# Hybrid streaming encoder step: output stores moved from ScalarE's queue to SP's, second x tile loaded and scaled behind the first weights

## The chip, the cores and the metric

The kernel runs on one core of one Trainium2 chip. A core has a matrix engine (PE), three elementwise engines (DVE, ACT for ScalarE, POOL for GpSimd) and SP, which here only issues DMAs. Each engine takes its own instructions in the order in which the program lists them. The metric is the device time of one execution in microseconds (us); less is better.

## The reference

One layer is applied to 1024 prompt rows and, with cached state, to 64 sample rows, each of width 1024, all in float32. Cut to what matters:

```python
def _layer(x, ...):
    h = _rms_norm(x, norm1_g)
    parts = jnp.split(h @ w_in, ...)           # 1024 x 3080
    ...                                        # three mixers: gated delta net, gated MLP, windowed attention
    x = x + jnp.concatenate([o_a, o_b, o_c], axis=-1) @ w_out
    h = _rms_norm(x, norm2_g)
    x = x + (jax.nn.silu(h @ w_gate) * (h @ w_up)) @ w_down      # 1024 x 2816, twice, and 2816 x 1024
    return x, caches and states
```

The change touches the first lines (the norm of the first rows of x) and the last (the stores of the final x, `y_p` for the prompt and `y_s` for the sample).

## The kernel before

**Precision.** A float32 product is made of three reduced-precision ones: an operand is split into a rounded high part (`acopy` to `h`, on ACT) and the remainder (a subtraction to `l`, on DVE), and PE multiplies high by high, high by low and low by high. Weights pass from the loaded tile `wr` into `hw` and `lw`.

**Start.** Rows are treated in three segments. For the first segment `x_load` (L251) loads row tiles of 128 x 1024 into `xs`, `Weights.load` (L119) loads pieces of `w_in` into `wr` (three buffers), and `x_stat` (L290) makes the reciprocal root mean square of each row: Square with a sum on ACT (L293), then a multiply-add (L287) and a power (L288) on POOL. The first two row tiles are scaled in place on DVE (L317), transposed on PE (L303), multiplied by the norm's gain and split. `W.run(1)` splits the first piece of weights. A scheduler sets the order of each engine ahead of the run, up to the last stage (`manual_schedule`, L1888), where the engines keep the written order as it stands.

**End.** The down projection of the feed-forward block uses a Strassen-like scheme of seven products instead of eight. Its inner dimension is cut into blocks (`KB`, six of them, the last with a single piece), and in each block the sample rows and then four pairs of prompt row tiles (here pair 0 to 3) are worked off. In a pair there are seven steps (`STEPS`, here n0 to n6), each with an operand tile `w` of its own that SP loads from DRAM (`a_load`, L1764, from `hd`). In the last block a step is three matmuls, and an operand is 128 KB. Steps n0, n1 and n2 give partial sums: ACT copies them out of PSUM (L86) and POOL adds them to the output tile `yf` (L1817). Steps n3 to n6 finish the four half tiles of the pair: DVE adds them (`y_add`, L92), and `y_out` (L1782) stores the 128 x 512 half tile, 256 KB. PSUM banks tie the steps together: n2 and n4 write on in a bank that ACT has just copied out, n6 in one that DVE has just added.

**What orders the loads of the end.** `fetch` (L1866) writes one `a_load` into the program after each step. It keeps at most nine operands named in `AL` ; the sample operands of the six blocks are never taken out of `AL`, so in the last block the written lead of a load over its step is three steps. On the chip a load waits for its buffer to be free, for an older DMA of its semaphore to have landed, and for what stands ahead of it on SP, and for nothing else.

Of the kernel before, what the change touches and what calls it, by code (L numbers as in the profile page):

```python
# [12 lines left out]
ALU = mybir.AluOpType  # L13
# [40 lines left out]
def hybrid_step(ctx, tc, x_prompt, x_sample, cache_k, cache_v, st_gdn, st_conv, norm1_g, w_in, conv_w, a_log,  # L54
# [3 lines left out]
    V, A, G, T, SP = nc.vector, nc.scalar, nc.gpsimd, nc.tensor, nc.sync  # L58
# [17 lines left out]
    def sb(p, shape, tag, dt=F32, bufs=None):  # L76
        return p.tile(shape, dt, tag=tag, name=tag, bufs=bufs)

    def ax():
        return pp.tile([128, 512], F32, tag="ax", name="ax", bufs=6)  # L80
# [167 lines left out]
    def x_rows(s, t):  # L248
        t0, np_, ns = SEGS[s]
        return (x_prompt[0, t0 + 128 * t:t0 + 128 * t + 128, :], 128) if 128 * t < np_ else (x_sample[0], 64)  # L250

    xs_tiles = {}

    def x_load(s, t, q=G):
        src, r = x_rows(s, t)
        x = sb(xp, [128, DM], "xs", bufs=3)
        q.dma_start(out=x[:r], in_=src)
        xs_tiles[s, t] = x
# [7 lines left out]
    prm1 = sb(gp, [128, 390], "tr", bufs=9)  # L266
    A.dma_start(out=prm1[0:8, 0:128], in_=norm1_g[0].rearrange("(k p) -> k p", p=128))
    W.load()
    W.load()
    x_load(0, 1)  # L270
    W.load()
    x_load(0, 2, SP)
    SP.dma_start(out=cst[:, 192:], in_=cst_in[:, 192:])
# [10 lines left out]
    def gpow(out, in_, a, b, e):  # L284
        n = in_.shape[-1]
        r = in_.shape[0]
        G.tensor_scalar(out=out, in0=in_, scalar1=a, scalar2=b, op0=ALU.mult, op1=ALU.add)  # L287
        G.tensor_tensor(out=out, in0=out, in1=e[:r, :n], op=ALU.pow)  # L288

    def x_stat(x, r):  # L290
        jk = sb(wp, [128, DM], "xt2", BF16, bufs=2)
        ss = sb(cp, [128, 1], "ss", bufs=4)
        A.activation(out=jk[:r], in_=x[:r], func=AF.Square, accum_out=ss[:r])  # L293
        gpow(ss[:r], ss[:r], 1.0 / DM, EPS, mhalf)
        return ss
# [16 lines left out]
            acopy(h, t[:, :, :r])  # L312
            tt(xl[:, 4 * j:4 * j + 4, c0:c0 + r], t[:, :, :r], h.bitcast(F32), ALU.subtract)

    rstd = [x_stat(xs_tiles[0, t], 128) for t in range(2)]
    for t in range(2):
        first = V.tensor_scalar(out=xs_tiles[0, t], in0=xs_tiles[0, t], scalar1=rstd[t], scalar2=None, op0=ALU.mult)  # L317
    pb = ax()
    T.transpose(pb[:, :8], prm1[0:8, 0:128], ident[0:8, 0:8])
    g1T = sb(cp, [128, 8], "g1T")  # L320
    V.tensor_copy(out=g1T, in_=pb[:, :8])
    ctx.enter_context(tc.issue_after(first.ins))
    W.run(1)
    prm = sb(gp, [128, 390], "tr", bufs=9)
    SP.dma_start(out=prm[0:8, 0:128], in_=norm2_g[0].rearrange("(k p) -> k p", p=128))
    SP.dma_start(out=prm[8:9, 0:128], in_=gdn_g)
# [1330 lines left out]
    D, AL, yf = {}, {}, {}  # L1657
# [124 lines left out]
    def y_out(t, h):  # L1782
        c = slice(512 * h, 512 * h + 512)
        dst = y_p[0, 128 * t:128 * t + 128, c] if t < 8 else y_s[0, :, c]
        A.dma_start(out=dst, in_=yf[t][:dst.shape[0], c])


    STEPS = ((0, "Y", ((0, 0, 0),)), (1, "Z", ((1, 1, 0),)), (2, "Y", ((0, 1, 0),)), (3, "X", ((0, 0, 1),)),
# [2 lines left out]
    def pair_steps(b, p):  # L1791
        kps, banks = KB[b], {}

        def step(n, bank, adds):
            fresh = bank not in banks
            if fresh:
                banks[bank] = mmb() if bank == "X" else ax()
            ps, a = banks[bank], AL.pop((b, p, n))
            m = 0
            for k, kp in enumerate(kps):  # L1800
                bh, bl = D[kp][RIGHT[n]]
                for l, r in ((a[:, 2 * k], bh), (a[:, 2 * k], bl), (a[:, 2 * k + 1], bh)):
                    T.matmul(ps, l, r, start=fresh and m == 0, stop=m == 3 * len(kps) - 1,  # L1803
                             skip_group_check=not fresh)
                    m += 1
                if p == 3 and n in LAST:
                    PT.give(D[kp][LAST[n], "h"], D[kp][LAST[n], "l"])
            WS.give(a)

            def add():  # L1810
                for i, j, done in adds:
                    t = PAIRS[p][2 + i]
                    if b + 1 == len(KB) and not done:
                        slot = WS.take()
                        c = slice(512 * j, 512 * j + 512)
                        acopy(block(slot), ps)
                        G.tensor_tensor(out=yf[t][:, c], in0=block(slot), in1=yf[t][:, c], op=ALU.add)  # L1817
                        WS.give(slot)
                        continue
                    y_add(t, j, ps)  # L1820
                    if done and b + 1 == len(KB):
                        y_out(t, j)
            later.append(add)
# [3 lines left out]
    def sample_steps(b):  # L1827
        kps = KB[b]

        def step(j):  # L1830
            ps, v = ax(), AL[b]
            m, last = 0, 4 * len(kps) - 1
            for k, kp in enumerate(kps):
                for i in range(2):
                    for w in D[kp]["B%d%d" % (i + 1, j + 1)]:
                        mm(ps, v[:, 2 * k + i], w, m == 0, m == last)
                        m += 1
            if j:
                WS.give(v)

            def add():
                slot = WS.take()
                tmp = block(slot)[:64]
                c = slice(512 * j, 512 * j + 512)
                acopy(tmp, ps[64:128, :])
                tt(yf[8][:64, c], ps[0:64, :], yf[8][:64, c], ALU.add)
                tt(yf[8][:64, c], tmp, yf[8][:64, c], ALU.add)
                WS.give(slot)
                if b + 1 == len(KB):
                    outs.append(lambda: y_out(8, j))  # L1850
            later.append(add)

        return [lambda j=j: step(j) for j in range(2)]
# [134 lines left out]
```

## Time and profile before

| | us |
|---|---|
| median of 3 runs | 1350.33 (1349.97 to 1350.61) |
| the profiled execution, its own time | 1349.63 |
| its span, first to last instruction | 1347.9 |
| PE busy in the span | 1311.6 |
| granted clock of PE, mean | 0.996 |

A row of the timeline reads: start and length in us, engine, line of the kernel, operation, tile written <- tiles read, shapes, how many instructions were put together (x3), and in brackets the idle time of the engine just before it and who ended it. ACTq and SPq are the two engines' instruction queues as they issue DMAs. A row of the DMA issues ends with the size of one and the median time from issue to landing.

### The profile page before, as it was taken

What the parts mean: (1) busy time and instruction counts of PE and PEld (TensorE: products, weight loads), DVE (VectorE), ACT (ScalarE), POOL (GpSimd) and SP (SyncE); (2) the same over time, 40 slices, a digit from 0 to 9 for tenths busy, and PEclk for the clock granted to TensorE, in tenths of its full rate; (3) what the DMA queues carried; (4) which work ended last, traced back from release to release, by engine and by line L of the source; (5) the groups of instructions that cost most, each with busy time, mean ns of one, the idle gap of its engine ahead of it and who ended that gap; (6) DMA issues with size and microseconds to landing.
All of it is one profiled execution on the core that took longest, in us unless ns stands there. A gap on an engine that the chain in (4) does not pass through costs nothing.

```text
span 1347.9 us, 26489 instructions
## 1 busy us (share of the span) xinstructions
PE 1311.6 (97%) x9922; PEld 1169.9 (87%) x9922; DVE 936.8 (70%) x2190; ACT 635.4 (47%) x1629; POOL 175.3 (13%) x250
## 2 busy tenths in 40 slices
PE   6999999999999999998999999999999988999997
PEld 6988888888878887788999999999999976777784
DVE  5887866756577675588866776667766687767764
ACT  7677455562555553546545554455544532222202
POOL 3101120100111110100000000000000333232104
PEclk9999999999999999999999999999999999999999
DMA  8975654434455573152533553345433499666645
GB/s 263 350 259 190 230 181 162 153 126 159 163 172 173 205 263 113 73 194 81 160 115 125 177 159 124 110 137 177 147 122 116 148 340 326 220 220 239 214 144 199
DMA packets 183075, 243.63 MB, mean 181 GB/s; under 512 B 14523, under 2 KB 133792, under 8 KB 182946
## 3 DMA queue, kind: packets, MB, share of 16 engines
q1 hardware_dynamic: 174754, 229.34, 51.6%
q10 hardware_dynamic: 6704, 8.36, 1.7%
q0 software_dynamic: 1488, 4.23, 1.0%
q8 instruction: 78, 1.28, 0.4%
q14 instruction: 51, 0.42, 0.1%
HBM read 160.92 MB, written 81.04 MB: 180 GB/s over the span
## 4 chain that ended last, share of the span: by engine, by line
PE 82%; DVE 6%; issue 6%; POOL 2%; DMA 2%; ACT 2%; POOLq 0%; ACTq 0%; DVEq 0%
PE ax L1490 29%; PE mm L95 25%; PE ax L95 11%; PE ax L1803 8%; PE mm L1490 5%; DVE x L92 2%; PE mm L1803 1%; DMA hd<-w 1%; PE ax L303 1%; PE ax L531 1%; DVE tr L89 1%; POOL x L1817 1%; PE ax L866 1%; POOL ssk L288 1%; DMA xs<-in_x_prompt_dram 0%
## 5 line engine op out<-in xcount | busy, mean ns | idle before, releaser
L1490 PE MATMUL ax<-x,w 128*128 128x256 f32 (+1 forms) x2552 | 358.6, 287 | 0.0
L1490 PEld LDWEIGHTS ax<-x,w 128*128 128x128 f32 x2552 | 334.2, 190 | 0.3 <-ACT x L86 0.2
L92 DVE TENSOR_TENSOR w<-w,w 128x512 fp32r<-128x512 f32 (+1 forms) x242 | 164.4, 687 | 88.4 <-PE ax L1490 52.7
L95 PE MATMUL mm<-xh,hw 128*128 128x384 f32 (+1 forms) x432 | 151.6, 351 | 0.0
L95 PE MATMUL mm<-xl,hw 128*128 128x384 f32 (+1 forms) x432 | 142.7, 330 | 0.0
L95 PE MATMUL mm<-xh,lw 128*128 128x384 f32 (+1 forms) x432 | 142.2, 329 | 0.0
L1803 PE MATMUL ax<-x,w 128*128 128x512 f32 x480 | 132.7, 401 | 7.8 <-DVE x L92 7.6
L92 DVE TENSOR_TENSOR x<-ax,x 128x512 f32<-128x512 f32 (+1 forms) x144 | 98.3, 687 | 58.6 <-PE ax L1803 48.3
L1803 PEld LDWEIGHTS ax<-x,w 128*128 128x128 f32 x480 | 91.7, 193 | 31.4 <-DVE x L92 11.4
L1490 PE MATMUL ax<-xr,w 128*128 128x288 f32 x616 | 116.1, 296 | 1.2 <-DVE s L92 1.2
L86 ACT ACTIVATE w<-w 128x512 fp32r<-128x512 f32 x154 | 94.9, 624 | 38.5 <-PE mm L1490 14.9
L1490 PEld LDWEIGHTS ax<-xr,w 128*128 128x128 f32 x616 | 94.9, 188 | 1.5 <-DVE s L92 1.5
L95 PEld LDWEIGHTS mm<-xh,hw 128*128 128x128 f32 x432 | 81.1, 188 | 9.6 <-issue 6.8
L86 ACT ACTIVATE s<-ax 128x256 f32<-128x256 f32 (+1 forms) x132 | 52.0, 394 | 75.7 <-PE ax L1490 75.2
L95 PEld LDWEIGHTS mm<-xl,hw 128*128 128x128 f32 x432 | 81.5, 189 | 0.8 <-issue 0.3
L95 PEld LDWEIGHTS mm<-xh,lw 128*128 128x128 f32 x432 | 81.0, 188 | 0.6
L1803 PE MATMUL ax<-f,w 128*128 128x512 f32 x220 | 72.5, 399 | 2.8 <-ACT w L86 1.5
L89 DVE SCALAR_TENSOR_TENSOR tr<-tr,cw 128x384 f32<-128x384 f32 (+1 forms) x108 | 64.1, 594 | 12.7 <-ACT tr L86 11.3
L1706 POOL TENSOR_TENSOR w<-x 128x512 f32<-128x512 f32 x6 | 8.8, 1463 | 488.4 <-PE ax L1490 442.2
L1490 PE MATMUL mm<-x,w 128*128 128x256 f32 (+1 forms) x528 | 70.5, 289 | 0.0
L1490 PEld LDWEIGHTS mm<-x,w 128*128 128x128 f32 x528 | 67.9, 190 | 0.2 <-issue 0.2
L95 PE MATMUL mm<-hw,xh 128*128 128x256 f32 (+1 forms) x216 | 62.6, 294 | 0.0
(360 smaller groups left out, 2489.9 us busy)
## 6 DMA issues: line engine op xcount, KB each, us to landing
hd<-e SPq DMA_DIRECT2D x140, 256.0 KB, 2.4
w<-hd SPq DMA_DIRECT2D x140, 256.0 KB, 4.3
lw<-wk SPq DMA_DIRECT2D x46, 512.0 KB, 4.5
hw<-wk SPq DMA_DIRECT2D x46, 512.0 KB, 3.7
wr<-in_w_in_dram SPq DMA_DIRECT2D x28, 512.0 KB, 5.9
wk<-hw SPq DMA_DIRECT2D x25, 512.0 KB, 3.8
wk<-lw SPq DMA_DIRECT2D x25, 512.0 KB, 3.9
w<-in_ffn_w_gate_dram SPq DMA_DIRECT2D x44, 256.0 KB, 3.3
```

The lines of the kernel that those rows point to most:

```text
L86: return A.activation(out=out, in_=in_, func=AF.Copy, scale=scale)
L89: return V.scalar_tensor_tensor(out=out, in0=in0, scalar=s, in1=in1, op0=op0, op1=op1)
L92: return V.tensor_tensor(out=out, in0=in0, in1=in1, op=op)
L95: return T.matmul(out, lhsT, rhs, start=start, stop=stop)
L288: G.tensor_tensor(out=out, in0=out, in1=e[:r, :n], op=ALU.pow)
L303: T.transpose(b[k // 4][:, (k % 4) * r:(k % 4) * r + r], x[:r, k * 128:k * 128 + 128], ident[:r, :r])
L531: T.transpose(b[u // 4][:, (u % 4) * 128:(u % 4) * 128 + 128], src(u).rearrange("p h i -> p (h i)"), ident)
L866: T.transpose(PTp[0:r0 + cnt, j, kv, :], P[:, kv, 128 * j:128 * j + r0 + cnt], ident)
L1490: T.matmul(ps[:, :NB[c]], a[:, k, :], b[:, k, :], start=first and i == 0, stop=i == 11, skip_group_check=not first)
L1706: eng.tensor_tensor(out=block(t), in0=a, in1=b, op=ALU.subtract)
L1803: T.matmul(ps, l, r, start=fresh and m == 0, stop=m == 3 * len(kps) - 1, skip_group_check=not fresh)
L1817: G.tensor_tensor(out=yf[t][:, c], in0=block(slot), in1=yf[t][:, c], op=ALU.add)
```

## The change

Three edits. `y_out` issues its stores on SP instead of on ACT. The second x tile is loaded on SP, between the first and the second piece of weights, instead of on POOL after the second. And the second tile's statistics and scaling are written behind the split of the first weights (`W.run(1)`), while `issue_after` now ties later DVE work to the first tile's scaling.

```diff
     W.load()
+    x_load(0, 1, SP)
     W.load()
-    x_load(0, 1)
     W.load()
...
-    rstd = [x_stat(xs_tiles[0, t], 128) for t in range(2)]
-    for t in range(2):
-        first = V.tensor_scalar(out=xs_tiles[0, t], in0=xs_tiles[0, t], scalar1=rstd[t], scalar2=None, op0=ALU.mult)
+    def x_first(t):
+        rstd = x_stat(xs_tiles[0, t], 128)
+        return V.tensor_scalar(out=xs_tiles[0, t], in0=xs_tiles[0, t], scalar1=rstd, scalar2=None, op0=ALU.mult)
+
+    first = x_first(0)
     pb = ax()
...
     ctx.enter_context(tc.issue_after(first.ins))
     W.run(1)
+    x_first(1)
...
-        A.dma_start(out=dst, in_=yf[t][:dst.shape[0], c])
+        SP.dma_start(out=dst, in_=yf[t][:dst.shape[0], c])
```

PE's order is the same before and after. On SP, in the last block, this is the stretch from pair 0's operand for n4 to pair 1's operand for n2, before:

```order
L1764 DMA w_16313<-hd 128x256
L1764 DMA w_16321<-hd 128x256
L1764 DMA w_16329<-hd 128x256
L1764 DMA w_16336<-hd 128x256
L1764 DMA w_16343<-hd 128x256
L1764 DMA w_16350<-hd 128x256
```

The same stretch of SP now, up to the first sample stores; w_16329 is what pair 0's n6 multiplies, w_16336, w_16343, w_16350 and w_16359 are pair 1's n0 to n3, x_14319 and x_14341 are pair 0's two output tiles:

```order
L1767 DMA w_16313<-hd 128x256
L1767 DMA w_16321<-hd 128x256
L1788 DMA out_dram<-x_14319 128x512
L1767 DMA w_16329<-hd 128x256
L1788 DMA out_dram<-x_14341 128x512
L1767 DMA w_16336<-hd 128x256
L1788 DMA out_dram<-x_14319 128x512
L1767 DMA w_16343<-hd 128x256
L1788 DMA out_dram<-x_14341 128x512
L1767 DMA w_16350<-hd 128x256
L1767 DMA w_16359<-hd 128x256
L1788 DMA out_dram<-x_14467 64x512 x2
```

The four stores of a pair, which wait for the sums after n3, n4, n5 and n6, now stand each ahead of an operand that is needed three steps on: the n6 operand of the same pair, then n0, n1 and n2 of the next. In the other pairs the order is the same, except that the sample stores come only here.

On ACT, before, the stores stood among the copies out of PSUM (pair 0's stores and pair 1's three copies):

```order
L1785 DMA out_dram<-x_14319 128x512
L1785 DMA out_dram<-x_14341 128x512
L1785 DMA out_dram<-x_14319 128x512
L1785 DMA out_dram<-x_14341 128x512
L86 ACTIVATE w_16356<-ax 128x512
L1785 DMA out_dram<-x_14467 64x512 x2
L86 ACTIVATE w_16367<-ax 128x512
L86 ACTIVATE w_16375<-ax 128x512
```

The same place of ACT now, with pair 1's three copies and the first two of pair 2:

```order
L86 ACTIVATE w_16356<-ax 128x512
L86 ACTIVATE w_16367<-ax 128x512
L86 ACTIVATE w_16375<-ax 128x512
L86 ACTIVATE w_16413<-ax 128x512
L86 ACTIVATE w_16422<-ax 128x512
```

ACT holds the copies alone, one behind the other; no store stands between them any more.

At the start of ACT's program (xs are the two x tiles, hw_154 and hw_148 the first piece of weights, hw_222 the second), as a piece of the difference:

```order
 L293 ACTIVATE xt_138,ss<-xs 128x1024
-L293 ACTIVATE xt_143,ss<-xs 128x1024
-L86 ACTIVATE hw_154<-wr 128x264 x4
+L86 ACTIVATE hw_148<-wr 128x264 x4
+L293 ACTIVATE xt_160,ss<-xs 128x1024
 L86 ACTIVATE hw_222<-wr 128x264 x4
```

The second tile's Square now stands behind the first weights' four copies; in the same way DVE's second scaling (L317) moved behind the four `lw` subtractions (L92). POOL's order keeps both multiply-adds (L287) ahead of both powers (L288), so the first tile's power still follows the second tile's Square. On SP the second x tile stands ahead of the second piece of weights, and the fourth piece, which waits for `lw`, moved ahead of five small parameter loads.

## Prediction

> **What bounds the kernel now.** I read the page first, then stages, then the timeline of the two ends. On the page PE is busy nearly throughout, so a change elsewhere counts only where PE waits.
>
> ```profile
> PE 1311.6 (97%) x9922; PEld 1169.9 (87%) x9922; DVE 936.8 (70%) x2190; ACT 635.4 (47%) x1629; POOL 175.3 (13%) x250
> ```
>
> Three stages of the end, as busy time of each engine in the stretch (then granted clock, DMA share, GB/s):
>
> ```profile
> 1310.00:1320.00 10.00, 9.99 (x44) 7.54 (x42) 6.33 (x9) 2.99 (x5) 1.67 (x2) 1.00 0.19 53
> 1326.00:1332.00 6.00, 4.13 (x18) 2.76 (x17) 2.77 (x4) 1.08 (x2) 2.92 (x3) 1.00 0.94 320
> 1338.00:1344.00 6.00, 5.12 (x19) 2.96 (x17) 2.38 (x5) 1.68 (x3) 3.82 (x3) 1.00 0.43 159
> ```
>
> Up to 1320 PE has no hole. In the last block it has: 1.9 us of six in the second row, 0.9 in the third. So what is moved there is on the path. Who makes the holes (ACT's rows, then PE's wait):
>
> ```profile
> 1320.80 3.49 ACTq L1785 DMA_DIRECT2D out_dram<-x  x4
> 1324.42 0.60 ACT L86 ACTIVATE w<-ax 128x512 f32<-128x512 f32 x1 [4.51 <-DVE x L92]
> 1326.04 1.19 ACTq L1785 DMA_DIRECT2D out_dram<-x  x2
> 1332.40 1.09 ACT L86 ACTIVATE w<-ax 128x512 f32<-128x512 f32 x2 [4.03 <-DMA out_dram<-x]
> PE ax L1803 <- ACT w L86: 3.2, 4, 1.7
> ```
>
> ACT's copies stand behind stores that wait for DVE's sums, and PE lost 3.2 us to late copies, in four waits, the longest behind the two sample stores at 1326.04. That is the most that freeing ACT can give back.
>
> SP's side, as its queue's rows and its waits:
>
> ```profile
> 1295.63 35.91 SPq L1764 DMA_DIRECT2D w<-hd  x28
> 1305.44 0.32 SPq L1764 DMA_DIRECT2D w<-hd  x1
> 1320.23 3.35 SPq L1764 DMA_DIRECT2D w<-hd  x7
> SPq L1764 <- DVE x L92: 3.7, 2, 2.9
> 1322.12 1.20 PE L1803 MATMUL ax<-f,w 128*128 128x512 f32 x4 [0.51 <-DVE x L92]
> ```
>
> The 28 rows are the 28 operands of the last block. The seventh, pair 0's n6, was issued at 1305.44 and used at 1322.12: a lead of 16.7 us in which any landing hides. SP does keep its order: the 14th load waited 2.9 us for a sum on DVE, until 1320.23, and the next six came in a row behind it, one per 0.48 us (3.35 / 7).
>
> **The stores on SP: what is late next.** Now each pair's store after n3 stands ahead of the same pair's n6 operand, and the stores after n4, n5, n6 ahead of the next pair's n0, n1, n2. A store waits for its sum, and with it everything behind: the lead of 16.7 us shrinks to three steps, less the sum, two issues and a landing. The path of one round, in rows of the last pair:
>
> ```profile
> 1336.51 1.20 PE L1803 MATMUL ax<-f,w 128*128 128x512 f32 x4 [0.17 <-DVE x L92]
> 1339.33 0.96 PE L1803 MATMUL ax<-f,w 128*128 128x512 f32 x3 [0.46 <-ACT w L86]
> 1341.08 0.69 DVE L92 TENSOR_TENSOR x<-mm,x 128x512 f32<-128x512 f32 x1 [2.87 <-PE mm L1803]
> 1341.80 3.07 ACTq L1785 DMA_DIRECT2D out_dram<-x  x4
> 1342.79 0.96 PE L1803 MATMUL ax<-f,w 128*128 128x512 f32 x3 [0.17 <-DVE x L92]
> 1344.53 0.34 ACTq L1785 DMA_DIRECT2D out_dram<-x  x1
> ```
>
> These are pair 2's n6 (with the first matmul of pair 3), pair 3's n2, the sum after n3, the first store, n6, and the last store. Call L the time from an operand's issue to its landing.
> - From n2's start to the store after n3: 1341.80 - 1339.33 = 2.47. Then 0.48 to the load's issue, then L. So n6 starts 2.95 + L after n2; before, 1342.79 - 1339.33 = 3.46. The load ends last as soon as L is over 0.51.
> - From n6's start to the store after it: 1344.53 - 1342.79 = 1.74; 0.48; L. So the next n2 starts 2.22 + L after n6; before, 1339.33 - 1336.51 = 2.82. The load ends last as soon as L is over 0.60.
> - A round is then 5.17 + 2L; before, 1342.79 - 1336.51 = 6.28. The operands of n0 and n1 follow earlier stores, and those of n3 to n5 come 0.48 apart behind n2's while PE takes 0.7 a step; none of them ends a path. The sample stores add two issues ahead of pair 1's n4; its n6, which waits for its own load, hides them.
> - Start: the first store was issued at 1320.80 and moves to SP at the same time. Pair 0's n6 starts at 1320.80 + 0.48 + L. Three rounds later pair 3's n6 starts at 1321.28 + L + 3 x (5.17 + 2L) = 1336.79 + 7L. It stood at 1342.79, so **the end moves by 7L - 6.00**. Behind n6 all is as before: sum, store, landing, now SP's.
>
> The gain on ACT is inside this: the copies are early, but n2 waits for its operand anyway.
>
> **How long is L.** Landing times in three stretches: loads of 128 KB with nothing else, the crowded end, and the last four stores:
>
> ```profile
> w<-hd SPq DMA_DIRECT2D x7, 128.0 KB, 2.1
> w<-hd SPq DMA_DIRECT2D x17, 128.0 KB, 3.8
> out_dram<-x ACTq DMA_DIRECT2D x4, 256.0 KB, 2.0
> ```
>
> No row has a 128 KB load right behind a 256 KB store in a calm stretch. Below, L is the 2.1 of a lone load: +8.7. Above, the 3.8 of the crowd, where seven loads a round are issued back to back beside the stores: +20.6. The new round moves 4 x 256 and 7 x 128 KB, 2.0 MB, in some 10 us, 200 GB/s, nearer to the row at 159 than to that at 320, so I go by the lone load plus its wait behind the store: 262 KB at 320 GB/s are 0.82 us, less the 0.48 between the issues, 0.3. **L = 2.4, and the end moves by 7 x 2.4 - 6.0 = +10.8 us.**
>
> Two rules of the Trainium skill bear on this, and they point apart. Its page "Perfetto Trace Analysis", section "DMA Optimizations", advises giving inputs one DMA-issuing engine and outputs another; by that rule the change mixes what stood apart, and it has no price for it. SP's 2.9 us wait with six loads behind it agrees.
>
> **The start.** Rows of the first 16 us:
>
> ```profile
> 7.84 1.06 ACT L293 ACTIVATE xt<-xs 128x1024 bf16<-128x1024 f32 x1 [2.05 <-DMA xs<-in_x_prompt_dram]
> 8.89 3.64 ACT L86 ACTIVATE hw<-wr 128x264 fp32r<-128x264 f32 x10
> L288 POOL TENSOR_TENSOR ss<-ss,mhalf 128x1 f32<-128x1 f32 x2 | 1.4, 711 | 0.1
> 9.95 1.58 DVE L317 TENSOR_SCALAR xs<-xs,ss 128x1024 f32<-128x1024 f32 x2 [4.33 <-ACT hw L86]
> 11.44 1.46 DVE L92 TENSOR_TENSOR lw<-wr,hw 128x264 fp32r<-128x264 f32 x4
> 12.81 1.28 DVE L92 TENSOR_TENSOR xt<-ax,g1T 128x512 f32<-128x512 f32 x2
> 15.09 0.39 PE L95 MATMUL mm<-hw,xl 128*128 128x264 f32 x1 [0.37 <-DVE xl L92]
> DMA packets 1349, 1.22 MB, mean 358 GB/s; under 512 B 560, under 2 KB 1221, under 8 KB 1349
> ```
>
> POOL takes both multiply-adds before both powers, so even the first tile's scaling (9.95) waits for the second tile's Square (7.84), before and after. The change therefore doesn't free the first tile; it puts four copies of weights (about 1.4 of ACT's 3.64 for ten) ahead of that Square. The last row is the traffic from 4.6 to 8.0: the second tile and the first weights shared it. Now the weights go first, and the tile lands at about the same 8.0, since together they are as many bytes; if the copies are done by then, Square starts 0.2 later. On DVE the four subtractions and the second scaling change places, and `xt` at 12.81 follows both either way. I take +0.4: 0.2 from the tile, and as much again for copies that are not done by then. Bounds: one tile's transfer, 0.52 MB at 358 GB/s, 1.5 us, earlier or later. Behind it the parameters that now stand behind the fourth weights (issued at about 12.9) are used no earlier than PE's transposes near 20, which hides them: a landing of up to 6 us would still be in time, and a longer one would cost what it is over.
>
> **Sum.** +10.8 and +0.4 on the profiled execution's 1349.63 is 1360.8; the median of the runs shown is 0.7 higher, so **1361.5**.
>
> **Rivals.**
> - *The loads hide, and ACT's freed copies pay.* If SP's loads kept their lead past a waiting store, PE would get back the 3.2 us it lost to ACT: 1350.3 - 3.2 + 0.4 = 1347.5, faster. It decides at L near 0.5 to 0.6 (above), or if the queue let loads pass. For it: PE's waits on ACT are real. Against: the shortest landing group is 2.0, and SP's loads did not pass the wait at 1320.23. The Trainium skill's page "DMA: Bandwidth & Descriptors", section "Issuing engines are not separate DMA queues", says that the issuing engine decides only where the sequencer's issue time is spent; by it alone this rival would hold, but no run here shows a store on SP that waits ahead of a load. Chance 0.06.
> - *It comes to nothing.* Lead lost and ACT's gain cancel: 7L - 6.0 near 0 needs L = 0.9, under half of any landing row. It would also be so if SP already ran only three steps ahead, but 16.7 us of lead speak against. 1350.5, chance 0.05.
> - *The crowd.* L stays at 3.8 because loads and stores now queue in one ring: +20.6, 1371. Against: 200 GB/s on average. Chance 0.07.
> - *The forecast,* L from 2.1 to 3.1: +8.7 to +15.7 with the start from -1.0 to +1.5. Chance 0.82.
>
> **How the numbers follow.** The forecast's own range is 1358 to 1368. I widen it below to 1356, for a path on which one of the seven landings is hidden (2.4 less), and leave it at 1368 above; the crowd and the two others, 0.18, stay out. About 0.2% (2.7 us) is what a measurement of this kernel can tell from no change. Slower is forecast and crowd, 0.89; same 0.05; faster 0.06.
>
> **What would show it.** Right: in the last block PE's waits are ended by DMA of `w`, twice a pair (n2 and n6), rounds of about 10 us in place of 6.28; SP's waits name DVE's sums; no copy on ACT is ended by `out_dram`. Landing of the operands near 2.4 makes the size right. Wrong: rounds of 6 us or less (the lead survived), PE's waits in other steps than n2 and n6, or a start that moved the first matmul by more than 1.5 us.

## The result and the profile after

The changed kernel took 1365.64 us (median of 4 runs, 1364.9 to 1368.74) beside 1350.47 for the kernel before (4 runs, 1349.97 to 1352.37). The ratio is 1.0114, with a 95% interval of 1.0096 to 1.0132: slower by 15.2 us, inside the predicted range and 4.1 us above the predicted 1361.5.

| | before | after |
|---|---|---|
| the profiled execution, its own time, us | 1349.63 | 1365.72 |
| its span, us | 1347.9 | 1363.9 |
| PE busy, us | 1311.6 | 1318.6 |
| granted clock of PE, mean | 0.996 | 0.988 |

The page of the changed kernel, first its busy row, then the group of matmuls that lost most. The last columns of a group are its busy time, the mean of one in ns, the idle time ahead of it and what ended most of that.

```profile
PE 1318.6 (97%) x9922; PEld 1173.2 (86%) x9922; DVE 936.5 (69%) x2190; ACT 637.1 (47%) x1629; POOL 176.2 (13%) x249
L1806 PE MATMUL ax<-f,w 128*128 128x512 f32 x220 | 77.4, 421 | 12.6 <-DMA w<-hd 12.4
```

Two things show. PE is idle 12.6 us ahead of these 220 matmuls (the page of before had 2.8), and a DMA of an operand ends nearly all of it. And the same number of matmuls is busy 7 us longer: PE did the same work, at a lower clock somewhere.

Where: SP's instruction queue in the last block, from the timeline of the changed kernel (L1788 are the stores, L1767 the operands):

```profile
1300.73 4.03 SPq L1767 DMA_DIRECT2D w<-hd  x3
1321.18 0.34 SPq L1788 DMA_DIRECT2D out_dram<-x  x1
1321.61 0.38 SPq L1767 DMA_DIRECT2D w<-hd  x1
...
1324.47 0.32 SPq L1767 DMA_DIRECT2D w<-hd  x1
...
1332.77 0.34 SPq L1788 DMA_DIRECT2D out_dram<-x  x1
1333.20 0.38 SPq L1767 DMA_DIRECT2D w<-hd  x1
...
1337.70 0.34 SPq L1788 DMA_DIRECT2D out_dram<-x  x1
1338.13 2.96 SPq L1767 DMA_DIRECT2D w<-hd  x4
1345.24 0.34 SPq L1788 DMA_DIRECT2D out_dram<-x  x1
1345.67 0.38 SPq L1767 DMA_DIRECT2D w<-hd  x1
...
1349.95 0.34 SPq L1788 DMA_DIRECT2D out_dram<-x  x1
1350.38 1.82 SPq L1767 DMA_DIRECT2D w<-hd  x4
1355.43 0.34 SPq L1788 DMA_DIRECT2D out_dram<-x  x1
1355.87 0.38 SPq L1767 DMA_DIRECT2D w<-hd  x1
```

From about 1304.8 to 1321.18 SP did nothing: the first store waited for its sum, and pair 0's n6 operand, which before was issued at 1305.44, stood behind it until 1321.61. PE's timeline in the same stretch; in brackets the idle time just before, and what ended it. The rows are n6 of pair 0, pair 1's n0, n1 and n2, then n6, n0, n2, n6, n2 and n6 of the pairs that follow:

```profile
1324.14 1.14 PE L1806 MATMUL ax<-f,w 128*128 128x512 f32 x3 [2.17 <-DMA w<-hd]
1325.73 0.79 PE L1806 MATMUL ax<-f,w 128*128 128x512 f32 x1 [0.45 <-DMA w<-hd]
...
1327.96 0.79 PE L1806 MATMUL ax<-xr,w 128*128 128x512 f32 x1 [0.59 <-DMA w<-hd]
...
1329.40 1.48 PE L1806 MATMUL ax<-f,w 128*128 128x512 f32 x3
...
1336.00 0.94 PE L1806 MATMUL ax<-f,w 128*128 128x512 f32 x3 [2.68 <-DMA w<-hd]
1337.83 0.47 PE L1806 MATMUL ax<-f,w 128*128 128x512 f32 x1 [0.89 <-DMA w<-hd]
...
1341.52 1.62 PE L1806 MATMUL ax<-f,w 128*128 128x512 f32 x3 [0.93 <-DMA w<-hd]
...
1348.06 1.14 PE L1806 MATMUL ax<-f,w 128*128 128x512 f32 x3 [1.84 <-DMA w<-hd]
...
1352.99 0.94 PE L1806 MATMUL ax<-f,w 128*128 128x512 f32 x3 [0.58 <-DMA w<-hd]
...
1358.60 1.40 PE L1806 MATMUL ax<-f,w 128*128 128x512 f32 x3 [2.34 <-DMA w<-hd]
```

From n6 to n6 a round takes 11.86, 12.06 and 10.54 us; the last one before took 6.28, and 9.97 was predicted. Three matmuls in a row take 0.94 us at 1352.99 and 1.48 at 1329.40: the clock again. The stretches of the same kernel say so directly (start and end, length, busy time and count of PE, PEld, DVE, ACT and POOL, then PEclk, DMA share and GB/s):

```profile
1324.00:1328.00 4.00, 2.82 (x7) 1.36 (x7) 0.69 (x1) 0.59 (x1) 0.00 (x0) 0.59 0.67 219
1328.00:1332.00 4.00, 4.00 (x10) 2.97 (x11) 0.00 (x0) 1.20 (x3) 2.94 (x3) 0.56 0.65 189
1332.00:1336.00 4.00, 1.32 (x6) 0.78 (x5) 2.07 (x3) 0.00 (x0) 0.95 (x1) 1.00 0.55 168
1336.00:1340.00 4.00, 3.11 (x9) 1.77 (x9) 0.69 (x1) 0.60 (x1) 0.24 (x1) 0.80 0.59 195
1340.00:1344.00 4.00, 3.07 (x8) 2.02 (x7) 0.00 (x0) 1.20 (x2) 2.47 (x3) 0.50 0.42 133
```

In the second row PE is never idle and finishes 10 matmuls in 4 us; at full clock it finishes about 18 (44 in the 10 us from 1310 to 1320 before). The two stretches of the last block that were shown of before had 1.00. The prediction has no term for this. The waits of the changed kernel from 1315 on, PE's row, and SP's from 1300 on (total, times, longest):

```profile
PE ax L1806 <- DMA w<-hd: 13.0, 10, 2.7
```

```profile
SPq L1788 <- DVE x L92: 35.9, 12, 16.3
```

The start, in rows that answer to those of before: Square of the second tile, the first scaling, the first matmul, and the first one with the low part of x:

```profile
7.91 1.04 ACT L293 ACTIVATE xt<-xs 128x1024 bf16<-128x1024 f32 x1
9.98 0.75 DVE L317 TENSOR_SCALAR xs<-xs,ss 128x1024 f32<-128x1024 f32 x1 [4.33 <-POOL ss L288]
14.22 0.37 PE L95 MATMUL mm<-hw,xh 128*128 128x264 f32 x1
14.97 0.39 PE L95 MATMUL mm<-hw,xl 128*128 128x264 f32 x1 [0.26 <-DVE xl L92]
```

Square moved from 7.84 to 7.91, the first scaling from 9.95 to 9.98, and the matmul at 15.09 before to 14.97. The start moved by 0.12 us at most.

### The profile page after: what moved, and what is told of

Its sections match the earlier page's. It is cut to its first block, busy times and chain, and to the rows that moved or that the text cites. A ratio compares the mean times of both kernels' runs of the same rounds, so it can differ in the third digit from the quotient of the medians.

```text
span 1363.9 us, 26493 instructions
## 1 busy us (share of the span) xinstructions
PE 1318.6 (97%) x9922; PEld 1173.2 (86%) x9922; DVE 936.5 (69%) x2190; ACT 637.1 (47%) x1629; POOL 176.2 (13%) x249
## 4 chain that ended last, share of the span: by engine, by line
PE 81%; DVE 7%; issue 6%; POOL 2%; ACT 2%; DMA 1%; SPq 0%; DVEq 0%; ACTq 0%; POOLq 0%
PE ax L1493 28%; PE mm L95 24%; PE ax L95 10%; PE ax L1806 9%; PE mm L1493 5%; DVE x L92 2%; PE mm L1806 2%; DVE tr L89 1%; PE ax L303 1%; PE ax L534 1%; POOL x L1820 1%; DMA w<-hd 1%; DVE w L92 1%; PE ax L869 1%; POOL ssk L288 1%
## 5 line engine op out<-in xcount | busy, mean ns | idle before, releaser
L92 DVE TENSOR_TENSOR w<-w,w 128x512 fp32r<-128x512 f32 (+1 forms) x242 | 164.7, 688 | 88.8 <-PE ax L1493 54.5
L92 DVE TENSOR_TENSOR x<-ax,x 128x512 f32<-128x512 f32 (+1 forms) x144 | 98.6, 688 | 65.0 <-PE ax L1806 55.8
L1806 PE MATMUL ax<-f,w 128*128 128x512 f32 x220 | 77.4, 421 | 12.6 <-DMA w<-hd 12.4
L1806 PEld LDWEIGHTS ax<-f,w 128*128 128x128 f32 x220 | 42.3, 197 | 28.0 <-DVE x L92 6.9
```

Source lines behind the costliest of these rows:

```text
L92: return V.tensor_tensor(out=out, in0=in0, in1=in1, op=op)
```

## The experiments

Two theories stood at first. **Lead:** the loss is the lead of the operands, cut to three steps because stores that wait for sums stand ahead of them in SP's order. **Traffic:** the loss is that loads and stores share one queue, so that landings are slow, whatever their order. Later a third question came: what the slow clock costs. Every time is a median beside the kernel before on the same chip in the same series (1349.8 to 1350.7 in all of them), the ratio with its 95% interval. The ratio on record is not the quotient of the two medians; the two differ most for the stores alone (1.0103 and 1.0120).

| kernel | median, us | ratio | interval |
|---|---|---|---|
| the start alone | 1351.05 | 0.9997 | 0.9986 to 1.0007 |
| the stores alone | 1366.68 | 1.0103 | 1.0084 to 1.0122 |
| change, narrow stores | 1359.55 | 1.0065 | 1.0050 to 1.0080 |
| change, lead 4 | 1356.99 | 1.0047 | 1.0033 to 1.0062 |
| change, lead 5 | 1353.09 | 1.0016 | 1.0007 to 1.0025 |
| change, lead 6 | 1351.90 | 1.0008 | 0.9999 to 1.0018 |
| change, lead 9 | 1347.65 | 0.9972 | 0.9961 to 0.9984 |
| stores alone, lead 9 | 1347.05 | 0.9974 | 0.9962 to 0.9987 |
| before, lead 9 | 1349.12, 1349.63 | 0.9988, 0.9989 | 0.9976 to 0.9999, 0.9980 to 0.9999 |
| change, fillers before n2, n6 | 1365.34 | 1.0116 | 1.0096 to 1.0135 |
| change, fillers before n0, n1, n6 | 1362.70 | 1.0092 | 1.0079 to 1.0106 |

### Each part alone

The start's edits with the stores left on ACT:

```diff
-        SP.dma_start(out=dst, in_=yf[t][:dst.shape[0], c])
+        A.dma_start(out=dst, in_=yf[t][:dst.shape[0], c])
```

> The start of the change alone: the second x tile on SP between the weights and its scaling behind the first split; the output stores stay on ACT. If the loss is made by the stores that wait on SP (the queue), this takes the time of before within 0.1%, 1350 us, with first projection matmuls within 0.3 us of 14.2 and 15.0, and the last block's rounds stay at 6.28. If part of the 15 us comes from the start, for instance from parameters or weights that arrive late behind it, some of it stays here: 1352 us or more.

Then the kernel before with only the stores moved:

```diff
-        A.dma_start(out=dst, in_=yf[t][:dst.shape[0], c])
+        SP.dma_start(out=dst, in_=yf[t][:dst.shape[0], c])
```

> The other part of the change alone: the stores on SP, the start as before. The queue theory expects all of the loss here, +14 to +17 us over before (1364.5 to 1367.5), with PE's waits ended by DMA of w in n2 and n6 of each pair and a clock of PE that falls to a half for some 15 to 25 us of the last 40. If the start has a share, this is faster than the whole change by that share.

The start alone can't be told from no change, and the stores alone cost as much as the whole change. The loss is all in the last block. Single runs of the stores alone spread from 1361.73 to 1367.38, and the clock goes with them: the two fastest have a mean of 0.991 and 0.994 over the run, the other three 0.987 to 0.990. The fastest is the profiled one, and of four stretches of 4 us that begin at 1324, 1328, 1332 and 1336, three are at 0.96 or above; the second and the fourth:

```profile
1328.00:1332.00 4.00, 3.09 (x12) 1.92 (x12) 1.82 (x3) 0.60 (x1) 2.24 (x2) 1.00 0.53 157
1336.00:1340.00 4.00, 3.54 (x10) 2.33 (x10) 0.00 (x0) 1.19 (x2) 1.94 (x2) 0.62 0.63 198
```

That hint was followed below with the fillers.

### Lead or traffic

The whole change, with the loads written nine steps ahead instead of three. The sample operands are taken out of `AL` when they are used, so they no longer count against the limit of nine:

```diff
-                WS.give(v)
+                WS.give(AL.pop(b))
```

> The whole change, with the sample operands taken out of the list that limits fetch, so that in the last block a load is written nine steps ahead of its step in place of three. The stores stay on SP and wait there for the same sums. The queue theory says that a load behind a waiting store is harmful only because just three steps lie between; with nine (some 6 us of PE) the loads land in time, PE's waits on DMA of w go away, and ACT, freed of the stores, gives back up to the 3.2 us that PE lost to it: 1347 to 1349 us, faster than before. The rival, that stores and loads on one ring slow each other whatever their order, expects loads to land late still and the time to stay at 1360 or above.

And the whole change with three steps, but hardly any store traffic: only the first 16 of each 512 columns are stored, and the other 496 columns of the prompt and sample outputs are left unwritten:

```diff
-        SP.dma_start(out=dst, in_=yf[t][:dst.shape[0], c])
+        SP.dma_start(out=dst[:, 0:16], in_=yf[t][:dst.shape[0], 512 * h:512 * h + 16])
```

> The whole change, but each store writes only the first 16 of its 512 columns, so that most of the prompt's and the sample's output is left out: the wait on SP is the same, the traffic of the stores is gone (8 KB in place of 256 KB). The queue theory expects most of the loss to stay: a lone load's landing of 2.1 us in place of 2.4 to 3.2 in each of seven landings, so 3 to 5 us less than the whole change, 1360 to 1363. The rival, that the traffic of the stores on the same ring makes the loads late, expects the loss to be gone for the most part: 1352 or less.

With nine steps the loss is gone, and the kernel is 0.28% faster than before. PE's waits in its last block:

```profile
PEld ax L1806 <- DMA w<-hd: 1.6, 2, 1.1
...
PE ax L1806 <- DMA w<-hd: 0.6, 1, 0.6
```

Of PE's 13.0 us of waits for operands 0.6 are left; its weight loads (PEld) add 1.6. Its landings did not get faster for that. The DMA view of this kernel from 1321 to 1345 (mean rate, then the operands' median time from issue to landing):

```profile
DMA packets 4769, 6.57 MB, mean 274 GB/s; under 512 B 544, under 2 KB 2592, under 8 KB 4768
w<-hd SPq DMA_DIRECT2D x16, 128.0 KB, 3.6
```

The same view of the changed kernel, which is slower and so spreads its bytes over more time:

```profile
DMA packets 3330, 4.22 MB, mean 176 GB/s; under 512 B 384, under 2 KB 2176, under 8 KB 3328
w<-hd SPq DMA_DIRECT2D x14, 128.0 KB, 2.7
```

So the fast kernel has the slower landings, 3.6 against 2.7, and hides them. With narrow stores 6.1 of the 15.2 us went and 9 stayed, although a landing was then about that of a lone load:

```profile
w<-hd SPq DMA_DIRECT2D x17, 128.0 KB, 2.2
out_dram<-x SPq DMA_DIRECT2D x11, 8.0 KB, 1.5
```

The theory of traffic falls as the cause: it asked for 1352 or less. Traffic sets only the size: the working gives 7 x 2.2 - 6.0 = 9.4 for these landings, and 9.1 was measured. What the bytes are worth was a little more than expected (1359.55, where 1360 to 1363 was put down); the clock may count in it too, with a mean of 0.992 to 0.994 in the four runs against 0.985 to 0.989 in the changed kernel, so the 6 us need not all be landings.

### How long a lead is enough

The limit of `fetch` was set to four, five and six, in the kernel with nine (each of the three differs in this number alone):

```diff
-        if wants and len(AL) < (7 if hid else 9):
+        if wants and len(AL) < (7 if hid else 4):
```

> The whole change with a written lead of four steps in place of three. By the same working with an L of 2.4: each store stands ahead of a load needed four steps on; the next n0's operand lands 2.47 + 0.48 + 2.4 = 5.35 us after n2 (PE would be there at about 4.4), the next n2's 1.04 + 0.48 + 2.4 = 3.9 us after n6 (PE: 2.82 before). A round is 3.46 + 3.9 = 7.4 us, the end moves by about 3 to 4 us, and the time is 1352 to 1356. If the loss came from stores and loads sharing SP's queue at all, not from the lead, it stays near 1365; if any lead over three is enough, it is 1348.

> The whole change with a written lead of five steps. By the same working: the operand behind the store after n6 is the next n4's; it lands 1.74 + 0.48 + 2.4 = 4.6 us after n6, and PE needs it at 2.82 + 2 x 0.9 = 4.6. So nothing or next to nothing is late, rounds are 5.9 to 6.4 us, and the time is 1347 to 1350. If the price falls slowly with the lead (about 3 us a step from three to nine), it is 1358 to 1361.

> The whole change with a written lead of six steps. Corrected working, with the 3.7 us from issue to landing that the loads of the five-step version took in its denser traffic: the operand behind the store after n6 is the next n5's; it lands 1.74 + 0.48 + 3.7 = 5.9 us after n6, and PE needs it at 2.82 + 3 x 0.9 = 5.5; so at most 0.4 us is late a round. ACT's freed copies give back up to 3. Time 1347.5 to 1351, below the five-step version's 1353.1. If the loads' wait is set by the shared queue and not by the lead, it stays near 1353 or above.

The price falls with each step: +15.2, +6.5, +2.6 and +1.6 us beside before for three, four, five and six, and -2.8 for nine. The direction is that of the theory, but each of the three times came out above its range: by 1.0, by 3.1 and by 0.9 us. For four and five steps the step that failed is L = 2.4 as a constant. The same DMA view of the kernel with five steps:

```profile
DMA packets 4707, 5.93 MB, mean 247 GB/s; under 512 B 544, under 2 KB 3104, under 8 KB 4705
w<-hd SPq DMA_DIRECT2D x19, 128.0 KB, 3.4
```

A longer lead packs the same transfers closer, and they land later: 2.7 us at 176 GB/s (lead three), 3.1 at 208 (four), 3.4 at 247 (five), 3.6 at 274 (nine). At 3.4 the operand of the next n4 lands 1.74 + 0.48 + 3.4 = 5.6 us after n6 and is needed at 4.6, so each round is still late by 1.0. For six steps 3.7 was put into the expectation, and the time was still above it; the intervals of five and six overlap, so they are not told apart, and that of six contains 1, no change at all. Six steps are still 4 us from nine because the operands are still late: PE's waits for them in the last block of the six-step kernel are 4.0 us, where the nine-step kernel had 0.6:

```profile
PE ax L1806 <- DMA w<-hd: 3.4, 4, 1.3
PE mm L1806 <- DMA w<-hd: 0.6, 1, 0.6
```

The expectation looked only at the operand behind the store after n6, the next n5's. PE waits for that one twice (1.02 and 0.69 us), but also for an n4, an n3 and an n0 (1.34, 0.63 and 0.31). The limit counts in the earlier blocks as well, where it shortens the lead that they had, but nothing of the price lies there: the first store came at 1321.82, 1319.78 and 1321.59 with four, five and six steps, and at 1321.40 with nine.

### Whose gain is it at nine steps

Nine steps without the change's other parts: the kernel before with the same edit of `AL` (stores on ACT), twice, and the kernel before with that edit and the stores on SP.

> The kernel before with only the written lead of the operand loads made nine steps; the stores stay on ACT. If the lead matters only because stores stand ahead of loads on SP, this changes nothing: SP's loads hid before, PE still loses some 3 us to ACT's late copies, and the time is within 0.1% of before (1349.5 to 1351.5). The rival, that the nine-step version is fast because of its longer lead alone, whoever issues the stores, expects about 1347.7 here too.

> The nine-step lead with the stores on ACT once more, beside the same lead with the stores on SP. If moving the stores pays by itself once the loads are far enough ahead (ACT's copies no longer wait behind them), this is 1.0 to 3.2 us slower than its neighbour on SP; if the lead alone made the gain, the two are within 0.5 us.

> The kernel before with the nine-step lead and the stores on SP, its start untouched. If the start is worth nothing and the nine-step lead takes away the whole price of a waiting store, this is as fast as the whole change with that lead: 1346.5 to 1349, and 1.0 to 3.2 us faster than the same lead with the stores on ACT (1349.1 and 1349.6 in two series). If the start was part of that gain, or the lead alone made it, it is near 1349.5.

The lead alone is worth 0.11 to 0.12%, with the interval just clear of none; the first of the two times, 1349.12, is 0.4 below the range that took it for worth nothing. The rival that it makes the whole gain asked for 1347.7 and got 1349.1 and 1349.6. With the stores on SP as well it is 0.26 and 0.28%, with the start's edits and without them alike. What ACT still costs is seen in PE's waits of the nine-step kernel with its stores on ACT:

```profile
PEld ax L1803 <- ACT w L86: 6.3, 8, 1.8
PE ax L1803 <- ACT w L86: 2.8, 4, 1.4
```

The second row, 2.8 us, has no counterpart in the nine-step kernel with its stores on SP (above): there the copies are no longer late. About 2 us of difference in time (1349.1 and 1349.6 against 1347.65 and 1347.05) go with it. The intervals of the two pairs overlap a little, so the size is not sharp. Nor does every run with nine steps hide all landings: those with the start untouched spread from 1344.71 to 1351.55, and in the profiled one (1350.21) PE waited 2.4 us for operands, and its clock had 0.61 in the stretch from 1340 to 1344.

### What the slow clock costs

Eight matmuls into a spare PSUM bank ahead of n2 and n6 of each pair of the last block keep PE busy where it would wait. Their results are not used:

```diff
+            if b + 1 == len(KB) and n in (2, 6):
+                bh, bl = D[kps[0]][RIGHT[n]]
+                spare = mmb()
+                for _ in range(8):
+                    T.matmul(spare, bh[:, 0:128], bl, start=True, stop=True)
```

> The whole change, plus eight matmuls into a spare bank ahead of n2 and n6 of each last pair, which fill the wait for the operand and keep PE busy; their results are not used. If the half clock of the last block (17 us of it in the profile of the changed kernel) is set off by PE's holes and cost some 3 to 4 us, the clock stays near 1.0 there and the time is 1361 to 1363. If the slow clock is no part of the loss, or isn't set off by the holes, it is 1365 or more (the added 1.8 us at each place lies inside a wait of about 2.6).

This gave no answer. Pair 0's n2 doesn't wait for an operand, so the fillers ahead of it (some 1.8 us) delayed the first store, and with it all that follows. The profiled execution was the slowest of the four (1369.88), and in it the clock fell all the same, in the stretch from 1332; the other three, with a mean clock of 0.995 to 0.997, about that of before, took 1364.70 to 1365.77:

```profile
1332.00:1336.00 4.00, 4.00 (x12) 3.14 (x12) 0.00 (x0) 0.60 (x1) 1.95 (x2) 0.62 0.55 163
```

The fillers were then put only where PE's timeline of the changed kernel shows a wait:

```diff
+            if b + 1 == len(KB) and (n == 6 or p and n < 2):
+                bh, bl = D[kps[0]][RIGHT[n]]
+                spare = mmb()
+                for _ in range(8 if n == 6 else 3):
+                    T.matmul(spare, bh[:, 0:128], bl, start=True, stop=True)
```

> The whole change, with fillers (matmuls into a spare bank, results not used) only where the changed kernel's PE waited for an operand: eight ahead of each last n6 (a wait of 2.3 to 2.8 us there), three ahead of n0 and of n1 in pairs 1 to 3 (0.8 to 1.0 us), none ahead of n2, so that pair 0's n2 no longer pays for them as it did in the run with fillers ahead of n2. If the half clock is set off by PE's holes, and costs some 3 us of the loss, the clock stays at 1.0 in the last block and the time is 1361 to 1364. If the clock holds and the time stays at 1365 to 1366, the slow matmuls lay in the shadow of the loads and cost nothing; if the clock falls to 0.5 all the same, the holes don't set it off.

The clock stayed at 1.00 in every stretch of 4 us from 1324 to 1356; the two in which the changed kernel had 0.59 and 0.56:

```profile
1324.00:1328.00 4.00, 3.30 (x14) 2.05 (x12) 0.69 (x1) 0.60 (x1) 1.28 (x1) 1.00 0.72 231
1328.00:1332.00 4.00, 3.13 (x14) 2.11 (x13) 0.89 (x2) 1.20 (x2) 2.54 (x2) 1.00 0.59 170
```

It took 1362.7 us (1362.21 to 1363.77): 2.9 less than the changed kernel (1364.9 to 1368.74), with 50 more matmuls (4 x 8 + 6 x 3) and the same order on SP. All four runs have a mean clock of 0.995 or 0.996. PE still waited 4.9 us for operands, 1.3 at the longest, in place of 13.0 and 2.7. So with most of the holes filled the half clock is gone, and it had cost about 3 of the 15 us; the intervals of the two ratios overlap a little (1.0106 and 1.0096), so the size is not sharp.

Which holes set it off is not shown; their length alone doesn't say. In the four-step kernel PE waited 7.4 us for operands, 1.9 at the longest, was busy for just half of the stretch below, and kept a clock of 1.00 in every such stretch up to its last matmul:

```profile
PE ax L1806 <- DMA w<-hd: 7.4, 9, 1.9
1324.00:1328.00 4.00, 2.02 (x7) 0.97 (x6) 0.93 (x2) 1.19 (x2) 1.29 (x1) 1.00 0.87 276
```

In the profile of the first fillers the clock fell behind three holes of 0.74 to 0.76 us. Nor does it take a store on SP: the start alone, with its stores on ACT, had 0.69 in the stretch from 1328 to 1332.

## Why the prediction was right, point by point

**What bounds the kernel: right.** The loss lies in the last block; the start and the stores alone show it.

**SP keeps its order, and a store holds back the loads behind it: right.** SP waited 16.3 us with the first store at the head of its queue, and the nine-step kernel, which changes only how far ahead the loads stand, turned +15 into -3.

**The path of a round: right in form.** n6 waits in every pair for the operand behind the store after n3, and SP's waits name DVE's sums. "None of them ends a path" was wrong for one operand: pair 1's n1, issued at 1324.47, started its matmul at 1327.96, 3.5 us later, and pair 1's n2 then came behind it without a wait of its own. PE also waited for n0's operand, in pairs 1 and 2 for instance (1325.73 and 1337.83). That is the sign which the prediction had named against itself, and it costs little: n6 to n2 in pair 1 took 5.26 us, where 2.22 + 2.4 = 4.62 was predicted.

**L = 2.4: too small.** From issue to the first matmul, the six operands that ended a path took 2.53, 2.80, 3.39, 2.39, 2.61 and 2.73 us (SP's and PE's rows above), 2.74 on average. Part of it is a term that the sum hadn't got: PE starts some 0.14 us after its operand has landed (pair 3's n6: issued at 1355.87, landed 2.60 later, started at 1358.60). The six legs together are 2.05 us longer from this.

**The fixed parts of 2.47 and 1.74: right at full clock, wrong at half.** From n2 to the store after n3 it took 3.37, 3.72 and 2.44 us (1329.40 to 1332.77, 1341.52 to 1345.24, 1352.99 to 1355.43). The last, at full clock, is the predicted 2.47; the other two ran in stretches at 0.56 and 0.50. This adds 2.1; the legs from n6 to its store that set the end (1336.00 to 1337.70 and 1348.06 to 1349.95, 1.70 and 1.89 against 1.74) add 0.1.

**The sum.** Pair 3's n6 was predicted at 1336.79 + 7 x 2.4 = 1353.59 and came at 1358.60, 5.0 late: 2.05 from L, 2.1 + 0.1 from the fixed parts at half clock, 0.64 from pair 1's n1, 0.38 from a first store that came at 1321.18 in place of 1320.80 (in the profiles of the four-, five- and six-step kernels it stands between 1319.78 and 1321.82, so this is no effect of the change that could be told), less 0.3 because a load follows its store by 0.43 to 0.44 and not by 0.48, six times. Behind n6 it took 0.3 more to the end, and the start's +0.4 was nothing. With the predicted 10.8 that makes the 16.1 between the two profiled executions (1365.72 - 1349.63). The mechanism was right; the terms that were mis-sized are L, and a clock that the sum took for constant. No part of the range stood for that clock: its 2 to 3 us fell into the room that was left for an L of up to 3.1, which is luck.

**The start: +0.4 was nothing.** Square moved by 0.07, not 0.4, and the matmul behind it came 0.12 earlier. The bound of 1.5 either way held.

**The rivals.** "The loads hide, and ACT's freed copies pay" predicted 1347.5, and it is what a nine-step lead gives: 1347.65. Its condition was that the loads keep their lead. The copies are freed in the changed kernel too, as ACT's timeline shows:

```profile
1327.41 0.60 ACT L86 ACTIVATE w<-ax 128x512 f32<-128x512 f32 x1 [7.14 <-PE ax L1806]
1351.44 0.60 ACT L86 ACTIVATE w<-ax 128x512 f32<-128x512 f32 x1 [7.67 <-PE ax L1806]
```

ACT is idle 7 us until PE has something to copy; no store ends a wait there any more. The gain was there and lay beside the path. By the rule of the Trainium skill's page "DMA: Bandwidth & Descriptors", section "Issuing engines are not separate DMA queues", the engine that issues a DMA decides only where the issue time is spent. Here the same stores issued by another engine made +15.2 us with a lead of three steps and about -2 with nine: the rule leaves out what a waiting DMA holds back behind it. The advice of the Trainium skill's page "Perfetto Trace Analysis", section "DMA Optimizations", that one engine for inputs and another for outputs may make sense, held at three steps and not at nine, where the fastest kernels of the table have both on SP. "The crowd" (3.8 us per landing) was wrong at three steps, and near to what the longer leads show (3.4 and 3.6).

## What to carry to other kernels

Before a DMA that waits for a result is moved to an engine that issues loads, look at which loads stand behind it in that engine's order, and compare the time from the wait's end through issue and landing with the time at which each is needed; the landing must be taken at the traffic of the new schedule, not the old one. If the loads can be written further ahead, do that first: at nine steps the move cost nothing, and what it was meant to free paid. Where PE gets holes, its matmuls may be slower behind them as well, so count the holes and the clock apart; three steps of lead cost 15 us here, of which the clock was about 3.

## What was not expected of the hardware

- PE's clock went to half behind short holes. The longest idle time ahead of a matmul in the last block of the changed kernel is 2.7 us, and the first slow matmuls stand behind holes of 2.17 and 0.45 us. The Trainium skill's page "TensorE: Matmul & The Clock Gate", section "HAM oscillation — how this bites in real kernels", gives the rule that PE should have no idle gaps above about 3.4 us; in this block shorter ones were enough. Filling most of them kept the clock at 1.00 and took 2.9 us off; in the four-step kernel holes of up to 1.9 us left it at 1.00, and what decides between the two is open.
- Four operand loads in a row took SP 2.96 us to issue at 1338.13 and 1.82 at 1350.38, with the same instructions. The operand that came first in the slow group had the longest way to its matmul, 3.39 us. The cause was not looked for.
